# Low halves of projection weights: from a VectorE subtraction to a negated copy on ScalarE and an accumulating DMA

## The chip, the cores and the metric

The kernel runs on 1 core of one Trainium2 chip, as one launch. The metric is the device time of one execution in microseconds (us). A change is judged by the difference of the medians of timed runs on the same chip.

## What is computed

One layer of a hybrid encoder block on x of 1024 tokens by 1024 channels, all in float32:

```python
xn = rmsnorm(x, norm1_g)
u = xn @ w_in                     # 1024 x 5632: q,k,v | f,i,q,g | gate_sb, gate_hg
o_sb = stick_breaking_attention(q_sb, k_sb, v_sb)       # 8 heads of 64
o_hg = rmsnorm(hgrn2_chunkwise(...)) * silu(g_hg)       # 4 heads of 128
g_a = sigmoid(gate_sb + bg[:1024]); g_b = sigmoid(gate_hg + bg[1024:])
merged = g_a * (o_sb @ w_o_sb) + g_b * (o_hg @ w_o_hg)
h = x + merged @ w_out
h = h + square(relu(rmsnorm(h, norm2_g) @ w_ff1)) @ w_ff2
out = rmsnorm(h, final_g)
```

## The kernel before

Every large product is done in the reduced format `float32r` with split operands: a float32 operand `a` is written as `hi + lo`, where `hi` is `a` rounded to float32r and `lo` is the rest. `three` (L538) issues three matmuls per 128-deep slice: hi·hi, hi·lo and lo·hi. The helper `hi_lo` (L162) makes the pair: `hi_copy` (L153) is a cast on ScalarE (ACT), recorded under L154, and `lo_sub` (L156) is a subtraction `src - hi` on VectorE (DVE), recorded under L159. Since all splits go through these helpers, the profile tells them apart by tile names, not by lines.

The weights of the projections come as `Unit`s (L431). `Unit.load` brings a [128, 1024] float32 tile (512 KB) into one of two buffers of the tag "raw" by a DMA on SyncE's queue (SP); all such loads are in one order on SP. `Unit.split` (L460) makes `hi` and `lo` in one of two buffers each of the tags "whi" and "wlo". With two buffers, one unit is being multiplied while the next is split. A raw buffer can be filled again when its readers, the cast and the subtraction, are done.

The projections form a stream of jobs (`Stream`, L483) whose matmuls fill TensorE (PE) between the steps of the attention and of the recurrence (the "fill" and the "main" lane). A job's start calls `split` for itself, then `prefetch` (L502): the next unit is split and the one after it is loaded. The jobs touched by the change, in order:

- `wqk3` to `wqk7`: q and k of attention heads 3 to 7 (`qk_item`, L691). They run beside the attention, 126 to 330 us.
- `wf`, `wq`, `wg` of the four recurrent heads (`hg_job`, L1082): `wf0` to `wg3`.
- `wga0` to `wga7`: `RawUnit` (L1377), gate projections done as a fast product with fewer multiplications. Such a unit has two raw tiles, `ra` and `rb`. `split` casts and subtracts for `ra` (tiles `wga7whi`, `wga7wlo`), and forms differences in `rb` by two further DVE subtractions (L1340); `split_t` splits half of `rb` into one tile, `wga7t`, [128, 512] hi and [128, 512] lo. These units are "late": the next unit is split only after the first third of the job (L1431 to L1435), and its casts are ordered behind that job's copy `p1` (`hi_behind`).
- `wo00` to `wo03`: weights of the attention's output (`sb_job`, L1472), 551 to 611 us. After them comes the gates' stage, whose first unit `gp[0]` loads its weights `wg0r` into the same raw buffers (L1522), forms differences of them on DVE (L1546, recorded under L1340), and is multiplied from 610 us on.

Beside them run, and are named below: in the attention, `vr` (L656), the values of a head, loaded from a scratch tensor by two DMAs on GpSimd's queue (POOL) and subtracted on DVE (L668); `wTl` (L1001) and `wTh` (L995), the low and high half of the transposed attention weights, made on DVE and ACT; `po` (L1014), the product with the values. In the recurrence, `sd` (sums over pairs, L1182) and the running state `k` (L1269, L1271), which DVE updates from `pkv` and which the product `pho` (L1289) reads.

Another step of the kernel already has an accumulating DMA in it: `early_whole` (L876) copies `hi` to a new tile `xw` on ACT and adds `lo` to it by a DMA on POOL's queue. Eight of these, [128, 1024] float32 from SBUF to SBUF, run between 50 and 90 us.

Each engine executes its instructions in one fixed order. A scheduler decides that order when the program is built, by the priority in which the code issues the instructions and by its own estimate of when operands will be there; `after(...)` adds an order without a wait. All DMAs that POOL issues share one queue.

Of the kernel before, what the change touches and what calls it, by code (L numbers as in the profile page):

```python
# [9 lines left out]
F32 = mybir.dt.float32  # L10
# [3 lines left out]
AF = mybir.ActivationFunctionType  # L14
ALU = mybir.AluOpType
# [24 lines left out]
def kernel(  # L40
# [19 lines left out]
    nc = tc.nc  # L60
# [14 lines left out]
    def slot(name, dt=F32):  # L75
        return spool.tile([P, 1024], dt, tag="s", name=name)
# [17 lines left out]
    def bank(name):  # L94
        return psum.tile([P, 512], F32, tag="p", name=name)
# [12 lines left out]
    def after(ins, earlier):  # L108
        if earlier is not None and earlier.ins is not ins.ins:
            tc.add_manual_dep(ins.ins, earlier.ins.name, NOSYNC, reason="issue order")  # L110
        return ins
# [30 lines left out]
    last_lo, attended, silu = [None], [None], [None]  # L142
    turns = {"on": False, "act": None, "dve": None}

    def in_turn(engine, ins):
        if turns["on"]:
            after(ins, turns[engine])
            turns[engine] = ins
        return ins

    hi_behind, hi_last, turn_hi = [None], [None], [None]

    def hi_copy(dst, src):  # L153
        hi_last[0] = after(in_turn("act", nc.scalar.copy(dst, src)), hi_behind[0])  # L154

    def lo_sub(dst, src, hi):  # L156
        return in_turn(
            "dve",
            nc.vector.tensor_tensor(out=dst, in0=src, in1=hi.bitcast(F32), op=ALU.subtract),  # L159
        )  # L160

    def hi_lo(h, l, src):  # L162
        hi_copy(h, src)
        return lo_sub(l, src, h)

    def mul(out, a, b):
        return nc.vector.tensor_tensor(out=out, in0=a, in1=b, op=ALU.mult)

    def halves():
        return ((i, slice(i * 512, (i + 1) * 512)) for i in range(2))  # L170
# [176 lines left out]
    class Quads:  # L347
# [34 lines left out]
        def split(self, i, kp, src, pr=0, n=4):  # L382
            if (i, kp) not in self.hl:
                self.hl[i, kp] = tuple(slot(f"sq{n_}{i}{kp}", F32R) for n_ in "hl")
            h, l = (self.part(t, pr, n) for t in self.hl[i, kp])
            self.last_lo = hi_lo(h, l, self.part(src, pr, n))
# [44 lines left out]
    class Unit:  # L431


        late = False
        roomy = ()

        def split_t(self):
            pass
# [21 lines left out]
        def split(self, upto=None):  # L460
            self.load(upto)
            self.hl = self.hl or []
            for i, r in list(enumerate(self.raw))[len(self.hl) : upto]:
                if self.wide:
                    h = slot(f"{self.name}h{i}", F32R)
                    l = slot(f"{self.name}l{i}", F32R)
                else:
                    h = wpool.tile([P, 1024], F32R, tag="whi", name=f"{self.name}h{i}")
                    l = wpool.tile([P, 1024], F32R, tag="wlo", name=f"{self.name}l{i}")
                lo = after(after(hi_lo(h, l, r), last_lo[0]), attended[0])  # L470
                if self.name == "wf1":
                    after(lo, silu[0])
                self.hl.append((h, l))

    def cols_unit(name, parts):

        dmas, c = [], 0
        for mat, c0, n in parts:
            dmas.append((c, n, mat[:, c0 : c0 + n].rearrange("(k p) c -> p k c", p=P)))
            c += n  # L480
        return Unit(name, [dmas])
# [61 lines left out]
    def proj_half(ps, hl, mov, nk, half, wcol=lambda k: k * P, ts=slice(0, 512)):  # L543
        wh, wl = hl
        for kt in range(nk):
            c = wcol(kt)
            xh, xl = (t[:, ts] for t in mov(kt, half))
            three(ps, wh[:, c : c + P], wl[:, c : c + P], xh, xl, kt == 0, kt == nk - 1)
            if kt % 2 == 1:
                yield  # L550

    def proj_jobs(group, acts):


        def body():
            for half in range(2):
                for name, unit, ep in group:
                    ps = bank(f"{name}_{half}")
                    yield from proj_half(ps, unit.hl[0], acts.mov, KT, half)
                    ep(ps, half)  # L560

        return st.add([u for _, u, _ in group], body)
# [113 lines left out]
    def qk_epilogue(h):  # L676
        def ep(ps, half):
            if half == 0:
                qk[h] = tuple(slot(f"{n}{h}", F32R) for n in ("QH", "QL", "KS"))
            QH, QL, KS = qk[h]  # L680
            cs = slice(half * 512, (half + 1) * 512)
            hi_copy(KS[0:64, cs], ps[64:128])
            hi_copy(QH[0:64, cs], ps[0:64])
            lo_sub(KS[64:128, cs], ps[64:128], KS[0:64, cs])
            last_lo[0] = lo_sub(QL[0:64, cs], ps[0:64], QH[0:64, cs])
            for Q in (QH, QL):
                nc.gpsimd.dma_start(Q[64:128, cs].bitcast(F32), Q[0:64, cs].bitcast(F32))

        return ep

    def qk_item(h):  # L691
        u = cols_unit(f"wqk{h}", [(W_IN, C_Q + h * DHS, DHS), (W_IN, C_K + h * DHS, DHS)])
        return f"pjqk{h}", u, qk_epilogue(h)

    class FirstUnit(Unit):
# [376 lines left out]
    def silu_epilogue(h, key):  # L1072
        def ep(ps, half):
            t = hg_slot(h, key, half)
            nc.scalar.activation(t, ps, AF.Sigmoid)
            silu[0] = mul(t, ps, t)

        return ep
# [3 lines left out]
    def hg_job(h, key):  # L1082
        c0, ep = {
            "f": (C_F, f_epilogue), "q": (C_QH, lambda h: silu_epilogue(h, "q")),
            "g": (C_GH, lambda h: silu_epilogue(h, "g")),
        }[key]
        u = cols_unit(f"w{key}{h}", [(W_IN, c0 + h * P, P)])
        j_hg[h] = proj_jobs([(f"pj{key}{h}", u, ep(h))], xn)

    def hg_jobs(h):  # L1090
# [248 lines left out]
    def sub(out, a, b):  # L1339
        return nc.vector.tensor_tensor(out=out, in0=a, in1=b, op=ALU.subtract)  # L1340
# [36 lines left out]
    class RawUnit(Unit):  # L1377
# [11 lines left out]
        def split(self):  # L1389
            if self.hl is not None:  # L1390
                return
            self.load()
            ra, rb = self.raw
            h, l = (
                wpool.tile([P, 1024], F32R, tag=t, name=f"{self.name}{t}") for t in ("whi", "wlo")
            )
            after(sub(rb, ra, rb), after(hi_lo(h, l, ra), last_lo[0]))
            sub(rb[:, 512:], rb[:, 512:], rb[:, 0:512])
            self.hl = [(h, l)]

        def split_t(self):
            if len(self.hl) == 1:
                t = slot(f"{self.name}t", F32R)
                self.hl.append((t[:, 0:512], t[:, 512:]))
                hi_lo(*self.hl[1], self.raw[1][:, 512:])

    raw_units = [RawUnit(cb) for cb in range(KT)]
    for u in raw_units[:2]:
# [41 lines left out]
    def load_g1(cb):  # L1450
        g1r[cb] = half(f"g1r{cb}")
        load(g1r[cb], gd[cb])
# [3 lines left out]
    def sum_forms():  # L1456


        yield from range(7)
        for i, m in enumerate((6, 5, 7, 3)):  # L1460
            for kp in range(2):
                forms[m, kp] = tuple(slot(f"gs{n}{m}{kp}", F32R) for n in "hl")
                for j, t in enumerate(forms[m, kp]):
                    load(t.bitcast(F32), formd[m, kp][:, j, :])
                yield
            if m == 7:
                gp[0].load()
                gp[0].load_sums()
        yield from range(8)
        gp[0].split()  # L1470

    def sb_job(cp):  # L1472
        src = W_OSB[:, cp * 256 : (cp + 1) * 256].rearrange("(k p) c -> p k c", p=P)
        unit = Unit(f"wo0{cp}", [[(0, 256, src)]])

        def body():
            if cp == 0:
                side.append(sum_forms())
            for j in range(2):
                cb = 2 * cp + j  # L1480
                if 1 < cb + 1 < KT:
                    load_g1(cb + 1)
                g1 = g1r[cb]
                for i, cs in halves():
                    ps = bank(f"pys{cb}_{i}")
                    for _ in proj_half(
                        ps, unit.hl[0], a_sb.mov, 4, i, lambda k: k * 256 + j * P
                    ):
                        next(side[0], None)
                        yield  # L1490
                    if i == 0:
                        mul(g1, ps, g1)
                        nc.gpsimd.dma_start(yd[cb][:, i, :], g1)
                    else:
                        y = half(f"ys{cb}")
                        nc.scalar.copy(y, ps)
                        nc.scalar.dma_start(yd[cb][:, i, :], y)

        return st.add([unit], body)
# [815 lines left out]
    for i, it in enumerate(items):  # L2315
# [19 lines left out]
        r = turn(*it, between)  # L2335
# [142 lines left out]
```

## Time and profile before

| | |
|---|---|
| three timed runs | median 1449.54 us (1448.26 to 1450.98) |
| the profiled execution | 1448.06 us, of which 1446.1 us are its span |
| PE busy | 1422.6 us, 98% of the span |
| DVE busy | 1088.6 us, 75% |
| ACT busy | 655.8 us, 45% |
| POOL busy | 181.5 us, 13%, DMA issues not counted |
| data moved by DMA | 253.98 MB |

A row of a group of instructions gives the line, the engine, the operation, `out<-in` by tile names (a number at the end of a name is left out in some views, so that `xw` stands for eight tiles), the count, and the duration as min/median/max in ns with the first and last start in us. A row of the time line gives start, duration and, in brackets, how long the engine had been idle and who ended that. "DMA to landing" is the time from the issue of a DMA to the arrival of its data. A row of the windows gives length, busy time of each engine with the number of instructions, TensorE's granted clock, the mean busy share of the 16 DMA engines, and GB/s.

### The profile page before, as it was taken

Reading aid. Unit: us, or ns where it says so; the run is one execution under the profiler, and the core shown is the slowest. Engines: PE = TensorE matmul, PEld = TensorE weight load, DVE = VectorE, ACT = ScalarE, POOL = GpSimd, SP = SyncE. Lnnn points to the kernel's source line nnn. Section 1 sums busy time; section 2 is a strip of 40 time slices with the busy share of each in tenths; the row PEclk is TensorE's granted clock in tenths of the full one; section 3 lists DMA queues with packets and bytes.
Section 4 is the critical chain, followed back from the end, with each engine's and each line's share of the span. In section 5 each row is a group of like instructions: output and inputs, shape, how many; then the busy total and the mean of one; then the engine's idle time right before and its main releaser. Section 6 shows DMA issues by size and latency. Waiting matters only on the chain. (4 is left out here: it accounts for less than half of the span.)

```text
span 1446.1 us, 18993 instructions
## 1 busy us (share of the span) xinstructions
PE 1422.6 (98%) x7038; PEld 1190.4 (82%) x7038; DVE 1088.6 (75%) x1528; ACT 655.8 (45%) x1050; POOL 181.5 (13%) x338
## 2 busy tenths in 40 slices
PE   8999999999999999999999999999999999999998
PEld 7778888888888878888887888888888888888886
DVE  6868898988677778587777898666666757768765
ACT  6465666663233233333343675444444433523343
POOL 3224232320000001100010300000000000000042
PEclk9999999999999999999999999999999999999999
DMA  8687555651124137945469515344445974776724
GB/s 273 143 273 244 110 135 98 105 124 32 57 66 124 37 119 256 345 154 177 142 206 305 197 59 171 133 148 161 153 153 203 354 259 173 261 273 245 277 101 182
DMA packets 164180, 253.98 MB, mean 176 GB/s; under 512 B 26828, under 2 KB 90872, under 8 KB 164088
## 3 DMA queue, kind: packets, MB, share of 16 engines
q1 hardware_dynamic: 142776, 190.63, 38.9%
q0 software_dynamic: 17568, 55.59, 14.6%
q10 hardware_dynamic: 3744, 6.56, 1.2%
q8 instruction: 55, 0.90, 0.2%
q14 instruction: 37, 0.30, 0.1%
HBM read 178.28 MB, written 74.45 MB: 175 GB/s over the span
## 5 line engine op out<-in xcount | busy, mean ns | idle before, releaser
L154 ACT CAST whid<-w 128x1024 fp32r<-128x1024 f32 x30 | 31.6, 1053 | 154.6 <-PE pm L131 86.7
L131 PE MATMUL pm<-wlod,sh 128*128 128x512 f32 x240 | 93.5, 389 | 0.0
L131 PE MATMUL pm<-whid,sh 128*128 128x512 f32 x240 | 93.4, 389 | 0.0
L131 PE MATMUL pm<-whid,sl 128*128 128x512 f32 x240 | 93.4, 389 | 0.0
L947 DVE TENSOR_TENSOR_SCAN rm<-rm,bits 128x512 f32<-128x512 f32 (+6 forms) x72 | 87.1, 1220 | 6.1 <-ACT rm L921 5.9
L131 PE MATMUL pm<-tl,sh 128*128 128x512 f32 (+1 forms) x210 | 81.3, 387 | 0.0
L131 PE MATMUL pm<-th,sl 128*128 128x512 f32 (+1 forms) x210 | 81.3, 387 | 0.0
L131 PE MATMUL pm<-th,sh 128*128 128x512 f32 (+1 forms) x210 | 81.3, 387 | 0.0
L159 DVE TENSOR_TENSOR wlod<-w,whid 128x1024 fp32r<-128x1024 f32 x30 | 36.7, 1224 | 58.6 <-ACT whid L154 58.4
L2077 POOL TENSOR_SCALAR fss<-fss 128x1 f32<-128x1 f32 x8 | 4.5, 562 | 562.2 <-ACT fsc L2072 561.6
L995 ACT ACTIVATE wTh<-pw,minus_one 128x512 fp32r<-128x512 f32 (+2 forms) x96 | 53.0, 581 | 38.5 <-PE pw L134 35.8
L159 DVE TENSOR_TENSOR sl<-sa,sh 128x1024 fp32r<-128x1024 f32 x56 | 68.3, 1219 | 1.0 <-ACT sh L154 1.0
L1001 DVE SCALAR_TENSOR_TENSOR wTl<-pw,wTh 128x512 fp32r<-128x512 f32 (+2 forms) x96 | 50.4, 546 | 15.5 <-ACT wTh L995 14.2
L154 ACT CAST sh<-sa 128x1024 fp32r<-128x1024 f32 x56 | 57.2, 1046 | 5.5 <-DMA sa<-ad 5.5
L131 PEld LDWEIGHTS pm<-wlod,sh 128*128 128x128 f32 x240 | 45.0, 188 | 9.9 <-DVE wlod L159 0.6
L131 PEld LDWEIGHTS pm<-whid,sl 128*128 128x128 f32 x240 | 45.1, 188 | 9.4
L131 PEld LDWEIGHTS pm<-whid,sh 128*128 128x128 f32 x240 | 45.1, 188 | 9.2
L131 PE MATMUL pX<-sql,t1h 128*128 128x512 f32 x128 | 50.0, 391 | 0.4 <-DVE sql L159 0.4
L131 PE MATMUL pX<-sqh,t1l 128*128 128x512 f32 x128 | 49.8, 389 | 0.0
L131 PE MATMUL pX<-sqh,t1h 128*128 128x512 f32 x128 | 49.8, 389 | 0.0
L131 PEld LDWEIGHTS pm<-tl,sh 128*128 128x128 f32 x210 | 39.5, 188 | 8.1
L131 PEld LDWEIGHTS pm<-th,sh 128*128 128x128 f32 x210 | 39.4, 188 | 8.0
(942 smaller groups left out, 4438.0 us busy)
## 6 DMA issues: line engine op xcount, KB each, us to landing
w<-in_w_ff_dram SPq DMA_DIRECT2D x72, 512.0 KB, 4.7
sa<-ad SPq DMA_DIRECT2D x56, 512.0 KB, 5.8
ad<-a SPq DMA_DIRECT2D x32, 256.0 KB, 4.4
ad<-s SPq DMA_DIRECT2D x16, 512.0 KB, 3.2
tw<-in_w_out_dram POOLq DMA_DIRECT2D x24, 256.0 KB, 4.8
vi<-in_w_in_dram SPq DMA_DIRECT2D x10, 512.0 KB, 5.3
x<-in_x_dram SPq DMA_DIRECT2D x8, 512.0 KB, 7.1
xw<-xnl POOLq DMA_DIRECT2D x8, 512.0 KB, 7.6
```

The source lines that it names most:

```text
L131: return pe(nc.tensor.matmul(*a, **k))
L154: hi_last[0] = after(in_turn("act", nc.scalar.copy(dst, src)), hi_behind[0])
L159: nc.vector.tensor_tensor(out=dst, in0=src, in1=hi.bitcast(F32), op=ALU.subtract),
L947: sc = nc.vector.tensor_tensor_scan(out=rr, data0=rr, data1=bits[:, 1024 - nk + a : 1024 - nk + b][:, ::-1], initial=rm[:, b : b + 1] if i ...
L995: nc.scalar.activation(th[:, 0:n, qs], src, AF.Identity, bias=minus_one),
L1001: nc.vector.scalar_tensor_tensor(out=tl[:, 0:n, qs], in0=src, scalar=-1.0, in1=th[:, 0:n, qs].bitcast(F32), op0=ALU.add, op1=ALU.subtract,),
L2077: nc.gpsimd.tensor_scalar(out=ssq, in0=ssq, scalar1=1.0 / D, scalar2=EPS, op0=ALU.mult, op1=ALU.add)
```

## The change

A new helper `hi_lo_sent` takes the place of `hi_lo` for the units listed above. `hi` is cast as before. A second ACT instruction writes `-src`, rounded to float32r, into the tile of `lo`; this is `-hi`. Then a DMA on POOL's queue adds `src` to it in place, so that the tile holds `src - hi`. In all 29 subtractions of [128, 1024] and 8 of [128, 512] leave DVE, and as many ACT instructions and POOL DMAs come in.

```diff
+    def hi_lo_sent(h, l, src):
+        hi_copy(h, src)
+        hi_last[0] = after(
+            in_turn("act", nc.scalar.activation(l, src, AF.Identity, scale=-1.0)), hi_behind[0]
+        )
+        nc.gpsimd.dma_start(l.bitcast(F32), src, accum_op=ALU.add)
...
     class Unit:
+        sent = False
...
-                lo = after(after(hi_lo(h, l, r), last_lo[0]), attended[0])
-                if self.name == "wf1":
-                    after(lo, silu[0])
+                if self.sent:
+                    hi_lo_sent(h, l, r)
+                else:
+                    after(after(hi_lo(h, l, r), last_lo[0]), attended[0])
...
     def qk_item(h):
+        u.sent = h > 2
...
     def hg_job(h, key):
+        u.sent = True
...
     class RawUnit(Unit):
-            after(sub(rb, ra, rb), after(hi_lo(h, l, ra), last_lo[0]))
+            hi_lo_sent(h, l, ra)
+            after(sub(rb, ra, rb), last_lo[0])
...
-                hi_lo(*self.hl[1], self.raw[1][:, 512:])
+                hi_lo_sent(*self.hl[1], self.raw[1][:, 512:])
...
     def sb_job(cp):
+        unit.sent = True
```

The helpers record other lines after the change: the negated copy is L171, the DMA L173. The order of the engines around the unit `wga7` shows what moves. On ACT, from the copy `p1` of unit 6 on, before:

```order
L1431 COPY p1_6_5191<-pga6_5194 128x512
L154 CAST wga7whi_5232<-wga7r0_5127 128x1024
L1432 DMA pd6_124<-p1_6_5191 128x512
L154 CAST wga7t_5238<-wga7r1_5129 128x512
L1441 ACTIVATE g1_6_5193<-pga6_5194,prm_93 128x512
```

and with the change:

```order
L1445 COPY p1_6_5222<-pga6_5225 128x512
L154 CAST wga7whi_5263<-wga7r0_5158 128x1024
L1446 DMA pd6_124<-p1_6_5222 128x512
L171 ACTIVATE wga7wlo_5264<-wga7r0_5158 128x1024
L154 CAST wga7t_5270<-wga7r1_5160 128x512
L171 ACTIVATE wga7t_5270<-wga7r1_5160 128x512
L1455 ACTIVATE g1_6_5224<-pga6_5225,prm_93 128x512
```

Both negated copies stand next to the casts that they belong to.

On PE at the start of unit 7's first product (`pga7`), where `wga7wlo` is first read, before:

```order
L131 MATMUL pga7_5311<-xnh00_245,wga7whi_5232 128x512
L131 MATMUL pga7_5311<-xnl00_246,wga7whi_5232 128x512
L131 MATMUL pga7_5311<-xnh00_245,wga7wlo_5233 128x512
L131 MATMUL pga7_5311<-xnh00_245,wga7whi_5232 128x512
L131 MATMUL pga7_5311<-xnl00_246,wga7whi_5232 128x512
```

and with the change:

```order
L131 MATMUL pga7_5344<-xnh00_245,wga7whi_5263 128x512
L131 MATMUL pga7_5344<-xnl00_246,wga7whi_5263 128x512
L131 MATMUL pho2_0_5360<-v2_4651,sc2_4653 128x128 x2
L131 MATMUL pho2_0_5360<-k2_4243,q2_4372 128x128
L131 MATMUL pho2_0_5360<-v2_4651,sc2_4653 128x128
L131 MATMUL pho2_0_5360<-k2_4243,q2_4372 128x128
L131 MATMUL pho2_0_5360<-v2_4651,sc2_4653 128x128
L131 MATMUL pho2_0_5360<-k2_4243,q2_4372 128x128
L131 MATMUL pga7_5344<-xnh00_245,wga7wlo_5264 128x512
```

Seven small matmuls of the recurrence (`pho2_0`) have moved ahead of the first matmul that reads the low half.

On POOL in the attention, around the loads of the values of head 4 (`vr4`; `wTh3` and `wTl3` are tiles of attention weights, `tw` are sums of weights that are worked out in DRAM), before:

```order
L1439 DMA pd0_118<-p14_0_1988 128x512
L978 MEMSET wTh3_3_4_2150 128x128
L978 MEMSET wTl3_3_4_2151 128x128
L1367 DMA tw_142<-in_w_out_dram 128x512 x2
L978 MEMSET wTh3_0_0_2187 128x128
L978 MEMSET wTl3_0_0_2188 128x128
L659 DMA vr4_2205<-vrows_98 128x8x64 x2
```

and with the change:

```order
L173 DMA wqk5l0_2066<-wqk5r0_1753 128x1024
L1453 DMA pd0_118<-p14_0_1992 128x512
L990 MEMSET wTh3_3_4_2155 128x128
L990 MEMSET wTl3_3_4_2156 128x128
L1380 DMA tw_142<-in_w_out_dram 128x512 x2
L173 DMA wqk6l0_2214<-wqk6r0_2070 128x1024
L990 MEMSET wTh3_0_0_2192 128x128
L990 MEMSET wTl3_0_0_2193 128x128
L670 DMA vr4_2210<-vrows_98 128x8x64 x2
```

The two accumulating DMAs of `wqk5` and `wqk6` now stand in this queue, one of them directly ahead of `vr4`. SP's order is the same before and after.

## The prediction

> **What bounds the kernel now.** I read the page's first part, then PE's waits, then windows by stage, then the tiles that the change touches. The page says:
>
> ```profile
> span 1446.1 us, 18993 instructions
> PE 1422.6 (98%) x7038; PEld 1190.4 (82%) x7038; DVE 1088.6 (75%) x1528; ACT 655.8 (45%) x1050; POOL 181.5 (13%) x338
> ```
>
> PE is the bound, with 23.5 us idle in the whole span. The change removes work from DVE, so it can give back only what PE loses to DVE or ACT in the stretch where the moved splits lie. Windows of that stretch (columns: length, PE, PEld, DVE, ACT, POOL, clock, DMA share, GB/s; the last is the stage behind it):
>
> ```profile
> 126.00:330.00 204.00, 199.84 (x1185) 172.80 (x1184) 177.42 (x248) 128.12 (x262) 59.97 (x137) 1.00 0.54 119
> 330.00:505.00 175.00, 174.68 (x981) 148.05 (x980) 134.07 (x268) 53.81 (x108) 8.50 (x13) 1.00 0.22 65
> 505.00:560.00 55.00, 53.39 (x321) 44.84 (x319) 46.83 (x87) 21.29 (x43) 7.20 (x8) 1.00 0.47 153
> 560.00:615.00 55.00, 55.00 (x320) 46.37 (x320) 32.59 (x65) 16.85 (x38) 7.81 (x12) 1.00 0.91 321
> ```
>
> Length less PE busy: 4.2 + 0.3 + 1.6 + 0 = 6.1 us. That is all that can be won. The waits of PE name most of it:
>
> ```profile
> PE po L131 <- DVE wTl L1001: 2.6, 4, 0.8
> PE sd L131 <- ACT sd_h L154: 1.3, 1, 1.3
> PE po L131 <- ACT wTh L995: 0.6, 2, 0.3
> ```
>
> **What is removed.** One subtraction of each size:
>
> ```profile
> L159 DVE TENSOR_TENSOR wga7wlo<-wga7r,wga7whi x1: 1219/1219/1219, 537.5 to 537.5; 128x1024 fp32r<-128x1024 f32 x1
> L159 DVE TENSOR_TENSOR wga7t<-wga7r,wga7t x1: 690/690/690, 541.5 to 541.5; 128x512 fp32r<-128x512 f32 x1
> ```
>
> DVE loses 29 x 1.22 + 8 x 0.69 = 40.9 us of work. Nearly all of it lay under PE. What reaches the end is the wait of `sd` (1.3 us: its operand stands in DVE's queue behind two of these subtractions, and I give it back whole) and part of the 2.6 us on `wTl`. There the subtraction left at most some of the waits' causes, and ACT, which makes `wTh` ahead of `wTl`, now has 1 us more in front; I take half, 1.3 us. Gain 2.6 us, between 0.5 and 6.1.
>
> **What is added on ACT.** The negated copy is not in the trace. Below it stands the cast of the same shape, 1.05 us (rows further down), above it two activations of half the width:
>
> ```profile
> L995 ACT ACTIVATE wTh<-pw,minus_one 128x512 fp32r<-128x512 f32 (+2 forms) x96 | 53.0, 581 | 38.5 <-PE pw L134 35.8
> ```
>
> that is 2 x 0.58 = 1.16 us. I take 1.05 for the large and 0.62 for the small: 29 x 1.05 + 8 x 0.62 = 35.4 us on an engine 45% busy, hidden beside PE except where the low half is needed at once.
>
> **What is added on POOL.** The accumulating DMA has a row: `xw`, same shape, SBUF to SBUF. One behind idle queues, then the first and the last of six issued in a row:
>
> ```profile
> L879 POOL DMA_DIRECT2D xw<-xnl x1: 883/883/883, 88.3 to 88.3; - x1
> DMA to landing us min/median/max: 4.6/4.6/4.6
> ...
> L879 POOL DMA_DIRECT2D xw<-xnl x1: 924/924/924, 50.3 to 50.3; - x1
> DMA to landing us min/median/max: 4.7/4.7/4.7
> ...
> L879 POOL DMA_DIRECT2D xw<-xnl x1: 855/855/855, 55.0 to 55.0; - x1
> DMA to landing us min/median/max: 14.7/14.7/14.7
> ```
>
> Alone it lands 4.6 us after issue; six take (55.0 + 14.7 - 50.3 - 4.7) / 5 = 2.9 us each behind one another. So a low half is ready 1.05 + 1.05 + 4.6 = 6.7 us after the start of its high cast, where it took 1.05 + 1.22 = 2.3 us if DVE was free. That is 4.4 us later.
>
> The Trainium skill's page "DMA: Bandwidth & Descriptors" (Anatomy of one DMA, SWDGE path) fits 2.0 us plus bytes over 436 GB/s for a DMA that GpSimd issues, an estimate of 3.2 us for 512 KB. By it each place below would be 1.4 us better and the sum would end 1 to 2 us under the time before. The row of `xw` says 4.6, so the fit misses something that adding costs, and I go by the row.
>
> Most units have 8 to 24 us between subtraction and first use, and the later landing is covered by PE's matmuls of the job before. Four places have less. Each time the cast's start and the first matmul on the low half:
>
> ```profile
> 463.01 1.05 ACT L154 CAST wf3h<-wf3r 128x1024 fp32r<-128x1024 f32 x1
> ...
> L131 PE MATMUL pjf<-xnh,wf3l x16: 389/389/397, 469.9 to 483.8; 128*128 128x512 f32 x16
> ...
> 520.97 1.05 ACT L154 CAST wga6whi<-wga6r 128x1024 fp32r<-128x1024 f32 x1
> ...
> L131 PE MATMUL pga<-xnh,wga6wlo x8: 388/394/397, 527.0 to 538.7; 128*128 128x512 f32 x8
> ...
> 534.85 1.05 ACT L154 CAST wga7whi<-wga7r 128x1024 fp32r<-128x1024 f32 x1
> ...
> L131 PE MATMUL pga<-xnh,wga7wlo x8: 389/389/389, 539.8 to 549.3; 128*128 128x512 f32 x8
> L131 PE MATMUL pgq<-xnh,wga7t x8: 389/396/476, 543.5 to 546.2; 128*128 128x512 f32 x8
> ```
>
> - `wf3`: 463.0 + 6.7 = 469.7 against 469.9. No wait, but its raw buffer is freed by the DMA of `wga4`, so I put 0.3 us (0 to 2).
> - `wga6`: 527.7 against 527.0: 0.7 us.
> - `wga7`: 541.6 against 539.8, 1.8 us; the seven small matmuls that now stand ahead cover some 0.8. I put 1.0 us (0 to 3).
> - `wga7t`: behind `wga7wlo` and the store `pd6` in POOL's queue, 544 to 545.5 against a third matmul at 544.0, itself 1 us later. 0.4 us (0 to 2).
>
> The fifth place is a chain, at the end of the stretch. The raw buffer of `wo03` is filled next by `wg0r`; that load waited for the subtraction and now waits for the DMA. Behind it stand, in DVE's order, two differences and then the state `k` of the recurrence, which PE reads:
>
> ```profile
> 583.14 1.05 ACT L154 CAST wo03h<-wo03r 128x1024 fp32r<-128x1024 f32 x1 [0.77 <-PE pys L131]
> ...
> SPq L139 <- DVE wo03l L159: 2.5, 1, 2.5
> ...
> L139 SPq DMA_DIRECT2D wg0r<-in_w_in_dram x3: 368/383/384, 578.4 to 585.5; - x3
> DMA to landing us min/median/max: 4.5/4.5/4.5
> ...
> 590.04 1.29 DVE L1340 TENSOR_TENSOR wg0r<-wg0r,wg0r 128x512 f32<-128x512 f32 x2 [0.17 <-DMA wg0r<-in_w_in_dram]
> 591.87 0.29 DVE L1269 COPY k<-pkv 128x128 f32<-128x128 f32 x1 [0.54 <-PE pkv L131]
> 592.20 2.33 DVE L1271 SCALAR_TENSOR_TENSOR k<-k,fc,pkv 128x128 f32<-128x128 f32 x6
> ...
> 596.92 0.39 PE L131 MATMUL pho<-k,q 128*128 128x128 f32 x2
> ```
>
> Then: 583.1 + 6.7 = 589.8 landed, + 4.5 load = 594.3, + 1.3 differences + 0.3 copy + 2 x 0.39 = 596.7, against 596.9. It just fits if the queues are idle. They are not quite, so I put 1.0 us. SP's other loads (`wor`, `pr`, `yr`) queue behind the waiting one, but are read 10 us later or more.
>
> **The queue in the attention.** All that POOL issues behind an accumulating DMA also comes later. The trace has this: the copies `QH`, 128 KB, land in 2.4 us, but 14.1 behind the six `xw`:
>
> ```profile
> L687 POOL DMA_DIRECT2D QH<-QH x16: 516/550/940, 32.7 to 279.4; - x16
> DMA to landing us min/median/max: 2.1/2.4/14.1
> ```
>
> With the change, the loads `vr` of the heads stand behind `wqk6`, `wqk7`, `wga1t`. Head 5 in the trace:
>
> ```profile
> L659 POOL DMA_DIRECT2D vr<-vrows x2: 1601/1610/1618, 234.9 to 235.8; - x2
> L668 DVE TENSOR_TENSOR vr<-vr x1: 675/675/675, 245.2 to 245.2; 128x512 f32<-128x512 f32 x1
> DMA to landing us min/median/max: 8.5/8.5/8.5
> ```
>
> It lands at 244.3 for a reader at 245.2; 2.9 us later DVE stands 2 us. DVE has 204 - 177 = 27 us of slack over this stretch, and each head loses a 1.2 us subtraction, so I let 0.5 us in all reach PE (0 to 6).
>
> **Sum.** New waits 0.3 + 0.7 + 1.0 + 0.4 + 1.0 + 0.5 = 3.9 us, less the gain of 2.6: +1.3 us. The profiled execution took 1448.06 us (span 1446.1), 1.5 below the runs' median of 1449.54; it becomes 1449.4, and the median 1450.8. About 0.2% (2.9 us) is what a measurement of this kernel can tell from no change, so this is none.
>
> **Rivals.**
> 1. *The chain through `wg0r` becomes a long wait* (slower). For it: the DMA engines are full just there:
>
> ```profile
> 584.00:588.00 4.00, 4.00 (x23) 3.36 (x22) 1.92 (x2) 1.65 (x4) 0.13 (x1) 1.00 1.10 364
> 588.00:592.00 4.00, 4.00 (x24) 3.49 (x24) 2.12 (x4) 0.00 (x0) 0.41 (x1) 1.00 1.11 370
> ```
>
> If the accumulation lands after 9 to 14.7 us in place of 4.6, PE stands 4 to 10 us at `pho`, not 1. It decides from a landing of about 5 us on. Against it: SP is itself held by the waiting load, which thins the traffic. Middle +6 us over the forecast, 1457. Chance 0.20.
>
> 2. *POOL's queue holds up the attention* (slower). Five heads' `vr` 2 us late each, DVE already 87% busy there: some 5 of the 10 us reach PE through `wTl`. 1455. Against it: PE now waits only 2.6 us for `wTl`. It decides if DVE stands at `vr` for more than its subtraction gave back. Chance 0.12.
>
> 3. *The gain comes whole* (faster). All of `po` and `sd`, 3.9 us and up to 6.1, and only 0.5 us of new waits, since ACT's and DVE's queues run earlier and the casts with them. Median 1445.5. For it: DVE's subtractions often stood several us behind other work (`wo00`, `wq1`), so that 4.4 us later is too much. Chance 0.20.
>
> 4. *POOL is held while it issues.* The issue of `vr` takes 1.6 us at 235 us in the row above, `xw` 0.9. If each accumulating DMA is issued 0.7 us late, the four waits above grow by 2.8 us: 1453.6. Against it: the six `xw` all took near 0.9 with DVE busy. Chance 0.05. The Trainium skill's page "SBUF — State Buffer" (the "DVE blocks DMA" trap) has this as a rule: a DVE operation in a two-port mode keeps GpSimd from writing descriptors. It also says that `tensor_tensor` has no such mode, and most of what DVE does here is of that kind; no run here shows more.
>
> The forecast keeps 0.43; its own range is 1447.0 to 1452.2.
>
> **Range and chances.** 1446.0 leaves out the better half of rival 3; 1459.0 leaves out the longer half of rival 1; together under 0.2. Faster 0.20 (rival 3), same 0.43, slower 0.37 (rivals 1, 2, 4).
>
> **What would show it.** Right: DVE busy near 1048 us, ACT near 691; PE's wait for `sd_h` gone; waits of PE for DMAs into `wga6wlo`, `wga7wlo`, `wga7t` of about 1 us each; landing of these DMAs near 4.6 us. Wrong: PE waiting for `k` at `pho` by several us (rival 1), DVE idle for `vr` (rival 2), or landings of 3 us and no new waits (rival 3). If PE's idle time between 126 and 615 us doesn't move by what the total moves, the whole account is wrong.

## The result and the profile after

The changed kernel takes 1462.2 us (median of six runs, 1459.37 to 1465.42) against 1449.44 us (six runs, 1448.26 to 1450.98): the ratio is 1.0087, with a 95% interval of 1.0071 to 1.0102. It is slower by 12.8 us; 1450.8 us were forecast, and the upper end of the range was 1459.0.

The page's first part and, of the windows by stage, the four of the stretch that the change touches (columns as before: length, PE, PEld, DVE, ACT, POOL, clock, DMA share, GB/s):

```profile
span 1463.7 us, 19101 instructions
PE 1429.7 (98%) x7038; PEld 1195.3 (82%) x7038; DVE 1051.7 (72%) x1491; ACT 687.0 (47%) x1087; POOL 213.5 (15%) x375
```

```profile
126.00:330.00 204.00, 200.59 (x1193) 174.08 (x1192) 166.71 (x237) 139.17 (x275) 72.36 (x150) 1.00 0.71 147
330.00:505.00 175.00, 171.13 (x952) 144.84 (x951) 115.05 (x246) 65.46 (x122) 22.34 (x30) 0.99 0.45 110
505.00:560.00 55.00, 49.81 (x267) 40.60 (x267) 34.48 (x71) 22.63 (x40) 9.09 (x11) 0.94 0.59 142
560.00:615.00 55.00, 52.27 (x321) 44.57 (x320) 27.74 (x64) 17.35 (x30) 8.23 (x12) 1.00 0.93 292
```

The work moved as the change says: DVE's busy time fell by 36.9 us, ACT's rose by 31.2. The profiled execution is the slowest of the six (1465.42 us); its span grew by 1463.7 - 1446.1 = 17.6 us. Of these, 1429.7 - 1422.6 = 7.1 us are PE being busy longer with the same 7038 matmuls, and 10.5 us are PE idle longer. The attention's stretch gained 0.8 us. Nearly all the idle time came between 330 and 615 us: length less PE busy is 3.9 + 5.2 + 2.7 = 11.8 us in the last three windows, where it was 1.9.

PE's waits after, longest first (total, times, longest):

```profile
PE pjf L131 <- DMA wf3l<-wf3r: 3.5, 1, 3.5
PE pho L131 <- DVE k L1282: 2.7, 1, 2.7
PE po L131 <- DVE wTl L1013: 2.4, 5, 1.1
PE sl L131 <- DVE pp L176: 2.4, 1, 2.4
...
PE pga L131 <- DMA wga7wlo<-wga7r: 1.5, 1, 1.5
...
PE pga L131 <- DMA wga6wlo<-wga6r: 0.9, 1, 0.9
```

The wait of `sd` is gone, those on `wTl` are nearly as long as before (2.6). New are 3.5 us at `wf3`, 2.7 at `pho`, 2.4 at `sl`, 1.5 and 0.9 at `wga7` and `wga6`. Three chains stand behind the largest ones.

**`wf3`: a unit that is late because the unit before it holds its buffer.** The load of `wf3` before the change:

```profile
L139 SPq DMA_DIRECT2D wf3r<-in_w_in_dram x1: 368/368/368, 456.3 to 456.3; - x1
...
DMA to landing us min/median/max: 3.7/3.7/3.7
```

It went out when DVE had formed the difference that reads the same raw buffer, and arrived at 460.0 us. The cast started only at 463.0, behind ACT's copy for `wga4`, so the load had 3.0 us to spare. With the change, what SP waits for ahead of the load, the transfer that it waits for, the load, the cast, the unit's own transfer and the matmul that waits:

```profile
SPq L139 <- DMA wga4wlo<-wga4r: 16.5, 1, 16.5
...
L173 POOL DMA_DIRECT2D wga4wlo<-wga4r x1: 864/864/864, 455.6 to 455.6; - x1
...
DMA to landing us min/median/max: 4.7/4.7/4.7
...
460.44 0.37 SPq L139 DMA_DIRECT2D wf3r<-in_w_in_dram  x1
...
467.09 1.05 ACT L154 CAST wf3h<-wf3r 128x1024 fp32r<-128x1024 f32 x1 [3.57 <-DMA wf3r<-in_w_in_dram]
...
L173 POOL DMA_DIRECT2D wf3l<-wf3r x1: 850/850/850, 469.4 to 469.4; - x1
...
474.06 0.50 PE L131 MATMUL pjf<-xnh,wf3l 128*128 128x512 f32 x1 [3.53 <-DMA wf3l<-wf3r]
```

SP stands until the transfer into `wga4wlo` has landed, and the load goes out 4.2 us later than before. It then takes 6.6 us in place of 3.7, with the transfer of `wga4t` (456.7 to 463.0 us) and the load of `wq3` (from 463.1) beside it. The 3.0 us to spare take up part of these 4.2 + 2.9 us, and the cast starts 4.1 us late. The unit's own transfer lands 6.9 us after the cast's start, which is just when PE read the low half before (469.9 against 463.0). So nothing takes up the 4.1 us. PE itself comes 0.6 us later than before, at 470.5, and waits 3.5 us.

**`sl`: differences that moved ahead in DVE's order.** DVE after, at the differences of `wga6`, and the matmul that waits for the steps behind them:

```profile
521.90 1.23 DVE L1353 TENSOR_TENSOR wga6r<-wga6r,wga6r 128x1024 f32<-128x1024 f32 x1 [5.09 <-DMA wga6r<-in_w_in_dram]
...
524.44 0.17 DVE L176 TENSOR_TENSOR pp<-pp 128x8 f32<-128x8 f32 x1
...
524.67 1.34 PE L131 MATMUL sl<-q,k 128*64 128x64 f32 x16 [2.43 <-DVE pp L176]
```

Before, these differences were ordered behind the unit's low half, and so behind the steps of `k`, `q` and `pp`. They are no longer ordered behind it and now stand two levels of these steps earlier, while the load of `wga6` comes later: the second of its two DMAs was issued at 508.0 us before and at 517.6 after, because SP stood 7.5 us for the transfer into `wga5wlo`. (Of these 9.6 us, 5.9 are the lateness of the whole program by then: PE comes to this `sl` at 522.2 us, before at 516.3.) DVE stands 5.1 us, and PE 2.4 of them.

**`pho`: the forecast's fifth place.** The transfer of `wo03`, and DVE waiting for the weights that are loaded into its buffer:

```profile
L173 POOL DMA_DIRECT2D wo03l<-wo03r x1: 896/896/896, 598.6 to 598.6; - x1
...
DMA to landing us min/median/max: 9.2/9.2/9.2
```

```profile
610.60 0.69 DVE L1353 TENSOR_TENSOR wg0r<-wg0r 128x512 f32<-128x512 f32 x1 [7.38 <-DMA wg0r<-in_w_in_dram]
...
612.67 0.28 DVE L1282 COPY k<-pkv 128x128 f32<-128x128 f32 x1
...
613.01 0.49 PE L131 MATMUL pho<-k,q 128*128 128x128 f32 x2 [2.73 <-DVE k L1282]
```

**The clock.** PE's matmuls ran slower behind some waits. Windows of 2 us behind the wait at `wf3`, and, as the counterpart, behind the one at `pho` (the eighth figure is the granted clock):

```profile
474.00:476.00 2.00, 1.94 (x8) 1.71 (x9) 0.86 (x1) 0.00 (x0) 0.85 (x1) 0.72 0.79 227
476.00:478.00 2.00, 2.00 (x11) 2.00 (x11) 0.78 (x2) 0.00 (x0) 0.00 (x0) 0.50 0.94 239
478.00:480.00 2.00, 2.00 (x11) 1.70 (x10) 2.00 (x7) 1.00 (x1) 0.00 (x0) 0.93 1.04 208
...
614.00:616.00 2.00, 2.00 (x12) 1.69 (x11) 1.82 (x5) 2.00 (x4) 0.00 (x0) 1.00 0.93 307
```

The clock is at 0.5 for 3.4 us and costs 1.7 us. In this execution it happened four times: behind `wf3`, `sl` and `wga7`, and once at 69 us, ahead of anything that the change touches. That is 6.7 of the 7.1 us by which PE is busy longer. The Trainium skill's page "TensorE: Matmul & The Clock Gate" (What's actually happening) describes it: PE's clock is halved by an activity monitor that looks at free-running windows of 3.4 us. The trace agrees in the length, 3.4 us; the condition is taken up at the end.

### The profile page after: what moved, and what is told of

The parts are those of the page before. It is cut to its first block, busy times and chain, and to the rows that moved or that the text cites. A ratio compares the mean times of both kernels' runs of the same rounds, so it can differ in the third digit from the quotient of the medians.

```text
span 1463.7 us, 19101 instructions
## 1 busy us (share of the span) xinstructions
PE 1429.7 (98%) x7038; PEld 1195.3 (82%) x7038; DVE 1051.7 (72%) x1491; ACT 687.0 (47%) x1087; POOL 213.5 (15%) x375
## 5 line engine op out<-in xcount | busy, mean ns | idle before, releaser
L131 PEld LDWEIGHTS pm<-th,sl 128*128 128x128 f32 x210 | 39.5, 188 | 8.0
```

The lines of the kernel that those rows point to most:

```text
L131: return pe(nc.tensor.matmul(*a, **k))
```

## The experiments

Twelve kernels, in three sets. Each was timed in five rounds beside the kernel before, each set on one chip. The ratio is to the kernel before; the last column is the ratio less one, times 1449.1 us.

| kernel | transfers kept for | ratio (95% interval) | us |
|---|---|---|---|
| the change | all | 1.0087 (1.0071 to 1.0102) | +12.6 |
| p_attn | wqk3-7, wga0, wga1 | 0.9993 (0.9984 to 1.0002) | -1.0 |
| p_hg | wf, wq, wg of four heads | 0.9993 (0.9984 to 1.0002) | -1.0 |
| p_gate | wga2-7 | 1.0012 (1.0003 to 1.0021) | +1.7 |
| p_wo | wo00-03 | 1.0022 (1.0013 to 1.0031) | +3.2 |
| hg_gate | p_hg and p_gate | 1.0064 (1.0052 to 1.0076) | +9.3 |
| no_wga4 | all but wga4 | 1.0044 (1.0029 to 1.0058) | +6.4 |
| diff_late | all | 1.0067 (1.0055 to 1.0079) | +9.7 |
| free_raw | all | 1.0076 (1.0063 to 1.0090) | +11.0 |
| attn_hg | p_attn and p_hg | 0.9999 (0.9990 to 1.0007) | -0.1 |
| neg_add | none, ACT's copies kept | 1.0019 (1.0010 to 1.0028) | +2.8 |
| wo012 | wo00-02 | 1.0002 (0.9994 to 1.0011) | +0.3 |
| closure | all but wga4, 6, 7, wo03 | 0.9992 (0.9983 to 1.0001) | -1.2 |

### The four parts of the change

A switch per unit, `sent`, chooses `hi_lo_sent` or the old `hi_lo`; with it off, the orders of the old kernel are kept too. For a gate unit (the other units likewise):

```diff
-            hi_lo_sent(h, l, ra)
-            after(sub(rb, ra, rb), last_lo[0])
+            if self.sent:
+                hi_lo_sent(h, l, ra)
+                after(sub(rb, ra, rb), last_lo[0])
+            else:
+                after(sub(rb, ra, rb), after(hi_lo(h, l, ra), last_lo[0]))
```

p_attn. Expected: 

> Only the five units wqk3 to wqk7 and the gate units wga0 and wga1 go by the accumulating transfer; the other 26 subtractions stay on VectorE. Theory (raw buffers are given back late, and only where the next load has no slack does PE wait): PE waited 3.4 us in 126:330 with the whole change and 3.9 us before, so this part is worth nothing: 1449.4, within 1.5 us. Rival (POOL's queue and the DMA traffic cost a little everywhere, in proportion to the number of transfers): 9 of 37 transfers, so about a quarter of the 12.8 us: 1452.5.

p_hg. Expected: 

> Only the twelve units wf, wq, wg of the four heads go by the accumulating transfer. Theory (late buffers): wf3's own low half is ready at 463.0 + 6.7 = 469.7 against a first use at 469.9, and its load is not late, because the gate unit wga4 ahead of it still gives its buffer back by the subtraction: PE waits under 1 us there, 1450 within 1.5 us. Rival (each unit's own landing is what PE waits for): the 3.5 us at wf3 stays, with 1.7 us of slower clock behind it, 1454.6.

p_gate. Expected: 

> Only the gate units wga2 to wga7 go by the accumulating transfer. Theory (late buffers and the moved differences): the waits at wga6 and wga7 (0.9 and 1.5 us) and the wait of sl on pp (2.4 us, VectorE standing at the differences of wga6) stay, with 1.7 us of slower clock once or twice; wf3 is loaded 4 us late but split on VectorE in time: 1455, between 1452 and 1458. Rival (own landings alone): the two waits at wga6 and wga7 only, 2.4 us, 1452.

p_wo. Expected: 

> Only the units wo00 to wo03 go by the accumulating transfer. Theory (late buffers): wo03 frees the buffer of wg0r, whose differences stand ahead of the state k in VectorE's order: PE waits 1 to 3 us at pho, 1452. Rival (the wait at pho with the whole change only came from the lateness of all that ran before it): no wait, 1449.5.

Measured: -1.0, -1.0, +1.7 and +3.2 us, in all +2.9 of the 12.6. (In p_attn 28 subtractions stay, not 26.) So POOL's queue and the traffic as such cost nothing in the attention, and `wf3` is as forecast where `wga4` stays on VectorE. Its wait in p_hg:

```profile
PE pjf L131 <- DMA wf3l<-wf3r: 0.3, 1, 0.3
```

p_wo has the wait at `pho`, 2.0 us, and 1.7 us of slower clock behind it. p_gate missed the theory's 1455 and came out at its rival's 1452: the waits at `wga6` and `wga7` are there, the one at `sl` is not, although the differences are moved in that kernel too. DVE waits only 1.6 us at them: it comes to them 2.4 us after the load of `wga6` goes out (at 510.8 us), and with the whole change 0.8 us ahead of it (at 517.6). In these two kernels the moved differences cost PE time only where the load is that late as well.

### Two parts together, and one unit taken out

hg_gate sets `sent` for both groups, no_wga4 for all units but `wga4`. Expected of hg_gate: 

> The twelve units of the heads and the gate units wga2 to wga7 together go by the accumulating transfer; wqk3 to wqk7, wga0, wga1 and wo00 to wo03 stay on VectorE. Theory (the two parts spoil each other: wga4's transfer holds the buffer that wf3 is loaded into, and wf3 then has its own transfer on top; wg3's transfer holds the buffer of wga6, whose differences block VectorE): PE waits 3.5 us at wf3, 2.4 at sl on pp, 2.4 at wga6 and wga7, with 1.7 us of slower clock twice, less the 1.3 of sd: 1459, between 1456 and 1462. Rival (the parts add): 1449.1 - 0.7 + 2.2 = 1450.6.

Expected of no_wga4: 

> The whole change, but wga4's two subtractions are left on VectorE, so that its raw buffers come free as before. Theory (wga4's transfer makes wf3 late): the 3.5 us at wf3 falls under 1 us and the slower clock behind it goes: 1462 - 3.0 - 1.7 = 1457.3. Rival (wf3 waits for its own transfer, behind ACT's and POOL's queues): no change, 1462.

Measured: +9.3 us where the parts alone make +0.7. The parts do not add; the theory's 1459 was met (1458.3). PE's waits in hg_gate:

```profile
PE pjf L131 <- DMA wf3l<-wf3r: 3.5, 1, 3.5
...
PE sl L131 <- DVE pp L176: 1.2, 1, 1.2
```

In no_wga4 two subtractions on DVE in place of two transfers, with `wga4`'s differences back behind its low half, give back 6 of the 12.6 us: the load of `wf3` goes out at 456.1 us again and PE waits 0.7 us for its low half.

```profile
L139 SPq DMA_DIRECT2D wf3r<-in_w_in_dram x1: 368/368/368, 456.1 to 456.1; - x1
...
PE pjf L131 <- DMA wf3l<-wf3r: 0.7, 1, 0.7
```

The theory had 4.7 us for it. Not all of the 6 us is `wf3`: the wait at `sl` is 1.6 us in place of 2.4, and the slower clock is missing behind `sl` and `wga7` too.

### The order of the differences

```diff
-            after(sub(rb, ra, rb), last_lo[0])
+            after(after(sub(rb, ra, rb), last_lo[0]), hi_last[0])
```

Expected: 

> The whole change, but the two differences of a gate unit are ordered behind the unit's negated copy, which puts them back where they stood in VectorE's order before (behind the steps of k, q and pp). Theory (VectorE stood 5.1 us at the early differences of wga6, and PE 2.4 us at sl for it): this wait and 1.7 us of slower clock go, the wait of sd on sd_h (1.3) may come back: 1458.5, between 1457 and 1461. Rival (the wait at sl came from all that was late before, not from the order): 1462.

Measured: +9.7 us, 1458.7, as the theory had it, but not by its path alone. The wait at `sl` is gone; yet the small tile, which waits for the differences, is now late at `wga4`, and the wait at `wf3` is shorter because PE comes to it later:

```profile
PE pgq L131 <- DMA wga4t<-wga4r: 2.5, 1, 2.5
...
PE pjf L131 <- DMA wf3l<-wf3r: 1.8, 1, 1.8
```

### Buffers freed at once, transfers kept

```diff
-        nc.gpsimd.dma_start(l.bitcast(F32), src, accum_op=ALU.add)
+        nc.gpsimd.dma_start(l.bitcast(F32), h.bitcast(F32), accum_op=ALU.add)
```

Expected: 

> The whole change, but the transfer adds the high half in place of the raw weight, so the raw buffer is free after ACT's negated copy; the low halves become zero, so the low part of the products is left out of the output. Each transfer has the same size, issue and landing as in the change. Theory (the late buffers, not the late low halves, cost the time): the waits at wf3, sl and pho go, 2.4 us at wga6 and wga7 stay: 1451, between 1449 and 1453. Rival (PE waits for the landings themselves): 1460 or more.

Measured: +11.0 us by the ratio, 1460.1 us (the median itself is 1458.5): 5.5 to 7 us over the theory's range, and near the rival's 1460. The theory's first half holds: the waits at `sl` and `pho` are gone and the one at `wf3` is 0.7 us. But new waits stand elsewhere:

```profile
PE pga L131 <- DMA wga6wlo<-wga6whi: 2.9, 1, 2.9
PE pjf L131 <- DMA wf2l<-wf2h: 1.9, 1, 1.9
```

The landings did not stay as they were, and the queues show why. A raw buffer now comes free at the same moment as the transfer is issued, so the next load starts beside it. SP's load of `wf3`, POOL's transfer of `wga4` and its landing, in free_raw:

```profile
454.15 0.37 SPq L139 DMA_DIRECT2D wf3r<-in_w_in_dram  x1
...
454.42 0.87 POOL L173 DMA_DIRECT2D wga4wlo<-wga4whi  x1 [17.28 <-ACT wga4wlo L171]
...
DMA to landing us min/median/max: 6.6/6.6/6.6
```

With the whole change this transfer lands in 4.7 us, since the load waits for it. The changed kernel has the other case too, with the raw tile as the source: `wq3`, where a load of `wg3` goes out 0.1 us ahead of the transfer at 474.2 us, lands in 6.7:

```profile
L173 POOL DMA_DIRECT2D wq3l<-wq3r x1: 850/850/850, 474.2 to 474.2; - x1
...
DMA to landing us min/median/max: 6.7/6.7/6.7
```

And in free_raw `wga7`, issued 3.2 us ahead of the next weights' load, lands in 4.6. So held buffers and slow landings are two faces of one limit: the load and the transfer, 512 KB each, either follow or slow each other. Freeing the buffers moved the wait from `wf3`, `sl` and `pho` to `wga6`, `wf2`, `wga4` and `wga7`.

### ACT's copies without the transfers

```diff
-        nc.gpsimd.dma_start(l.bitcast(F32), src, accum_op=ALU.add)
+        return in_turn(
+            "dve",
+            nc.vector.tensor_tensor(out=l, in0=src, in1=l.bitcast(F32), op=ALU.add),
+        )
```

Expected: 

> ACT makes the negated copies of the whole change, but VectorE adds the raw weight to them in place of the transfer, 37 additions where the subtractions stood. Theory (ACT's 35 us of copies lie under PE; what costs is the transfers): 1449.5, within 1.5 us. Rival (ACT's copies delay the casts that PE waits for): 1453 or more, with PE waiting for ACT.

Measured: +2.8 us, over the theory's range. PE's one much longer wait in it:

```profile
PE sd L131 <- ACT sd_h L154: 3.2, 1, 3.2
```

It was 1.3 us; the slower clock behind it costs another 2.8 in the profiled execution. ACT itself stands idle for `sd_x`, of which `sd_h` is cast; what is late is `sd_x` in DVE's order, and it becomes so at the low half of `wga6`. Before, then in neg_add:

```profile
522.05 1.23 DVE L159 TENSOR_TENSOR wga6wlo<-wga6r,wga6whi 128x1024 fp32r<-128x1024 f32 x1 [2.61 <-ACT wga6whi L154]
...
528.39 1.22 DVE L167 TENSOR_TENSOR sd_x<-k,q 128x1024 f32<-128x1024 f32 x1
```

```profile
524.73 0.69 DVE L1360 TENSOR_TENSOR p<-p,pgq 128x512 f32<-128x512 f32 x1 [3.83 <-PE pgq L131]
525.33 1.22 DVE L182 TENSOR_TENSOR wga6wlo<-wga6r,wga6wlo 128x1024 fp32r<-128x1024 f32 x1
...
531.72 1.22 DVE L186 TENSOR_TENSOR sd_x<-k,q 128x1024 f32<-128x1024 f32 x1
```

From the low half to `sd_x` it takes 6.3 to 6.4 us in both. The addition starts 3.3 us later than the subtraction did; 1.5 us of this is the program's lateness by then (its cast starts at 522.4 us, before at 521.0). Of the other 1.8 us about half is ACT's copy, which ends at 524.4, and half is `p`, which now stands ahead of the addition in DVE's order and waits for PE.

This chain is only in neg_add; in the changed kernel DVE waits for no copy, and in the stretch from 126 to 615 us PE waits for ACT only 0.6 us at `wTh`, as before. The rival's point, that the copies hold up casts in ACT's own order, is not borne out here; that ACT's copies cost nothing under all orders is not either.

### `wo03` alone, the two harmless parts, and the account closed

wo012 and attn_hg only set the switch. Expected of wo012: 

> Only wo00, wo01 and wo02 go by the accumulating transfer. Theory (wo03 alone cost the 3.1 us of the four, because wg0r is loaded into its buffer and k stands behind wg0r's differences): 1449.1, within 1 us, and no wait at pho. Rival (each of the four delays the loads behind it on SP, and wg0r is last of them): half or more of it stays, 1450.7 to 1452.

Expected of attn_hg: 

> The units wqk3 to wqk7, wga0, wga1 and the twelve units of the heads go by the accumulating transfer, wga2 to wga7 and wo00 to wo03 stay on VectorE. Theory (only gate units from wga2 on and wo03 hold buffers that are needed at once, so these two parts add): 1449.1 - 0.85 - 0.67 = 1447.6, faster than the kernel before by about 0.1%. Rival (parts spoil each other whenever two of them meet): 1450 or more.

closure sets it for all but `wga4`, `wga6`, `wga7` and `wo03`, and orders the differences as diff_late does. Expected: 

> The whole change, but wga4, wga6, wga7 and wo03 stay on VectorE, and the differences of the other gate units are ordered behind their negated copies. Theory (these four units and the moved differences are all that costs): 1449.5, between 1448 and 1451, PE's idle time in 330:615 within 2 us of before's. Rival (transfers and POOL's queue cost everywhere, and waits turn up at other units): 1453 or more.

Measured: wo012 +0.3, so nearly all of the 3.2 us was `wo03`. attn_hg is 0.1 us from the kernel before, with an interval that holds no change and just reaches the theory's 0.1% gain; it tells nothing more than that nothing is lost. closure keeps 30 of the 37 transfers and is at -1.2 us. Its windows:

```profile
330.00:505.00 175.00, 174.66 (x984) 147.99 (x983) 119.43 (x254) 65.88 (x122) 21.20 (x29) 1.00 0.43 104
505.00:560.00 55.00, 52.47 (x313) 43.92 (x311) 44.35 (x85) 22.66 (x45) 9.50 (x12) 1.00 0.61 167
560.00:615.00 55.00, 55.00 (x321) 46.38 (x320) 29.93 (x61) 17.81 (x39) 8.05 (x12) 1.00 0.98 345
```

PE's idle time between 330 and 615 us is 0.3 + 2.5 + 0 = 2.9 us, against 1.9 before and 11.8 with the whole change. One wait of the rival's kind does turn up at another unit (0.4 us of it in wo012 too):

```profile
PE pys L131 <- DMA wo00l<-wo00r: 1.2, 1, 1.2
```

Still, four units of 29, together with the order of the differences, carry the whole loss. How much `wga6`, `wga7` and the order carry each was not tried. closure beats the changed kernel by 14 us; that it beats the kernel before is not shown, as its interval reaches 1.0001.

## Why the prediction was wrong

The sign of the sum was right, and the size far off: +1.3 us in the forecast against +12.8. Its own terms, beside what they measured in the profiled execution:

| term | forecast | measured |
|---|---|---|
| `wf3` | 0.3 | 3.5 |
| `wga6`, `wga7` | 0.7, 1.0 | 0.9, 1.5 |
| `wga7t` | 0.4 | no wait listed (0.9 and 1.5 in hg_gate and p_gate) |
| `wo03` to `pho` | 1.0 | 2.7 |
| attention | 0.5 | -0.8, with `wTl` |
| `sl` behind the differences | not in the sum | 2.4 |
| slower clock | not in the sum | 6.7, of which 1.7 ahead of the change |
| gain at `sd`, at `wTl` | -1.3, -1.3 | -1.3, -0.2 (the 0.2 are part of the attention's 0.8) |

- **The step that failed** is "its raw buffer is freed by the DMA of `wga4`, so I put 0.3 us (0 to 2)": 3.5 us were measured. The link was named and then not worked out. Worked out with the prediction's own landing it would still have looked harmless: the cast of `wga4` at 452.2 us in the trace before, + 6.7 = 458.9, + 3.7 for the load = 462.6, ahead of the cast of `wf3` at 463.0. The runs showed two delays in its place. The transfer of `wga4` landed 7.8 us after the cast's start and not 6.7, since two copies of ACT's stand between cast and negated copy. And the load took 6.6 us and not 3.7, with other transfers beside it. That PE got the operand at 463.0 + 4.4 + 6.7 = 474.1 us is luck, since 4.4 has neither the 2.9 us of the slower load nor the 3.0 us to spare in it.
- **The unit's own landing was not it.** `wf2` has the same 6.9 us from the cast to the first use (396.9 to 403.8 us before) and is missing among the prediction's "Four places". Its load is in time in the changed kernel, and PE waits 0.2 us for it. For `wf3` it waits 0.3 us in p_hg and 0.7 in no_wga4, where the load is in time, and 3.5 in hg_gate and the changed kernel, where it is not.
- **Each late place was costed against the old times of all others.** Three of the twelve kernels show it: p_hg and p_gate make +0.7 us apart, and hg_gate, with both, +9.3. With two raw buffers, a transfer delays the load of the unit after next, and the delay reaches whichever unit has no slack left.
- **The moved differences were not seen.** They stand in the order of the changed program, two levels of the recurrence further ahead. In p_gate PE does not wait for them; behind a later load it waits 2.4 us.
- **The landing was right where the queues were idle**, 4.6 to 4.7 us at `wf3`, `wga6` and `wga7` against 4.6 from the row of `xw`; the fit of the Trainium skill's page "DMA: Bandwidth & Descriptors" (Anatomy of one DMA, SWDGE path) would have given 3.2, an estimate. Whether the adding makes the difference no run here shows. Where a load of 512 KB went out within 0.3 us, it was 6.7 to 7.0 us, and at `wo00` to `wo03` 5.5 to 10.7. The row of six in a row, 14.7 us for the last, had shown that transfers beside one another land late.
- **Rival 1** named the right chain at `pho`, and the landing of 9.2 us lay where it had to. Its price was less than the 4 to 10 us given: 2.7 us, and 2.0 in p_wo with a landing of 9.0. The load behind it landed in 3.4 us, in p_wo in 2.9, and not in 4.5, and PE went on after the copy of `k` alone. It was one of the five places, worth about 3 of the 12.6 us (p_wo), and not the main cause.
- **Rival 2** is refuted by p_attn: nine transfers and five heads' loads behind them, and nothing lost. DVE waits 8.5 us for `vr` in the changed kernel (1.4 before), and its slack covers them. Rival 3's gain is refuted by the change itself: relieving DVE by its subtractions left the waits on `wTl` at 2.4 of 2.6 us. Rival 4 has nothing for it: the issues take 0.85 to 0.96 us.
- **"Hidden beside PE"** for ACT's copies held in the changed kernel, and so did **the gain at `sd`**: the wait goes when the two subtractions of `wga6` leave DVE (p_gate has none), and is back with 1.3 us when they return (closure).
- **The forecast's own test** said that PE's idle time between 126 and 615 us must move by what the total moves. It moved by 9.1 us, and the span of the profiled execution by 17.6. Of the other 8.5 us, 7.1 are PE busy longer, nearly all of it the slower clock, which no part of the prediction priced; 1.4 are idle time elsewhere.

How the 12.8 us of the medians divide between waits and clock is an argument only: the profiled execution is 3.2 us over the median of its kernel, which is about two stretches of slow clock at 1.7 us.

## What to carry to other kernels

A transfer in place of an engine's instruction holds its source for its whole landing time. With two buffers in turn, add the landing to the load of the unit after next, take that load's own time beside the other transfers and not alone, add the unit's own landing, and follow the sum until slack takes it up; costing each unit against the old times misses the sum. Parts that cost 0.7 us apart can cost 9 together, so an account of a change to many units is tested by taking single units out (one unit gave back 6 of 12.6 us here). And an instruction that loses an ordering can move ahead in its engine's order, in front of work that did not wait before.

## What the hardware did that was not expected

PE's clock falls to half for 3.4 us behind some of its waits. Over the profiled executions of all fourteen kernels, from 20 us on, none of 60 waits between 0.9 and 1.5 us was followed by it, 15 of 31 waits between 1.5 and 2.9 us were, and all three of over 2.9 us. It costs 1.7 us each time (2.8 once, behind 3.2 us in neg_add).

The traces also show what decides among these. In all fourteen, any two changes of the clock lie a whole number of 3.413 us apart; in the changed kernel they are 18, 1, 118, 1, 14, 1, 7, 1 and 265 such steps. So the span can be cut into windows of 3.413 us. PE was idle for 1.9 us or more in 16 of them, and the clock fell at the end of each; between 1.66 and 1.88 us it fell in two of four, and below that in none. (The ends of matmuls are modelled, so the limit, about half a window, is rough.) Two such windows of the changed kernel, first the one that ends with the fall behind `wga7`, then the one with most of the wait at `pho`, without a fall behind it (the second figure is PE's busy time):

```profile
549.97:553.38 3.41, 1.75 (x11) 1.18 (x10) 3.38 (x8) 3.00 (x8) 1.45 (x2) 1.00 0.92 190
611.40:614.82 3.42, 1.81 (x13) 1.72 (x14) 3.12 (x8) 2.59 (x3) 0.00 (x0) 1.00 0.88 317
```

Of the 1.5 us at `wga7`, 1.4 lie in one window, with 0.3 us of other idle time; the 2.7 us at `pho` are split into 1.1 and 1.6. The wait of 2.0 us at 65 us stands in all fourteen executions, and the clock fell behind it in eight: where the windows lie is chance for the program. The page of the Trainium skill named above, "TensorE: Matmul & The Clock Gate" (What's actually happening), gives the condition as an idle window of about 3.4 us; here 1.9 us of idle time in one window were enough. A wait between 1.5 and 2.9 us, say of 2 us, is therefore worth about 2.8 us on average (2 + 15/31 x 1.7, an estimate), and one of 1.3 us only itself.

An accumulating DMA of 512 KB from SBUF to SBUF lands in 4.6 us alone. Between 280 and 530 us, where a load of 512 KB goes out within 0.3 us of it, it lands in 6.2 to 7.6 us (changed kernel and free_raw).
